# First norm's roots on every partition, from dense sums, in a two-layer decoder trunk

## The chip, the cores and the metric

The kernel runs on one core of a Trainium2 chip. The metric is the device time of one execution in microseconds (us); the span of a profile is the time between its first and last instruction, and the execution's own time is a little longer than the span. Engines are named as in the profile: PE (TensorE, with PEld for its weight loads), ACT (ScalarE), DVE (VectorE), POOL (GpSimd) and SP (SyncE, which here issues the DMAs).

## The reference

Two pre-norm residual layers over 256 tokens of width 1024. Layer 0 mixes tokens with forgetting attention, layer 1 with block-sparse attention; each is followed by a SwiGLU FFN and a gated embedding, and a last norm ends it. What matters here is the norm and its first use:

```python
def _rmsnorm(x, g):
    x32 = x.astype(jnp.float32)
    y = x32 * lax.rsqrt(jnp.mean(x32 * x32, axis=-1, keepdims=True) + RMS_EPS)
    return (y * g.astype(jnp.float32)).astype(x.dtype)
...
u = _rmsnorm(h, attn_norm_g[i])
...
proj = u @ fox_w_in[j]
q, k, v = _heads(proj[..., :D]), _heads(proj[..., D:2 * D]), _heads(proj[..., 2 * D:3 * D])
f_logit = proj[..., 3 * D:].astype(jnp.float32) + fox_b_f[j].astype(jnp.float32)
log_f = jax.nn.log_sigmoid(f_logit).transpose(0, 2, 1)
```

There are seven norms: three in each layer (before the mixer, the FFN and the embedding's gate) and the last one. The kernel numbers them 0 to 6.

## The kernel before, in words

The hidden state is held transposed in `hx`: 128 partitions by 8 blocks of features by 256 tokens. So a token's sum of squares runs over partitions, and a root per token is wanted in two shapes: as a row (the same 256 numbers on every partition, `row`) for results that have tokens along the free axis, and as a column (`col`, 128 tokens on the partitions, two columns) for results that have tokens on partitions. The norm's gain is put onto the input before the products, the root onto their results: products of queries, keys, values and gates start before the root is known.

Products are made in a three-fold split: each float32 operand is a high part (`whi`, made by ACT, line 186 or 162) and a low part (`wlo`, made by DVE, line 187 or 167), and `mm3` (lines 96 to 100) adds three products. Weights stream in as 216 blocks of 128 x 1024 (`half`, lines 142 to 188). SP issues their DMAs into six buffers `raw`, ACT and DVE split them into six pairs `whi` and `wlo`, and PE uses them in the order of the text. The tile framework puts each engine's instructions into an order by a planner of its own, by readiness and priority; so an instruction can stand elsewhere on ACT, DVE or SP than the text has it. Waits are semaphores, and each engine takes its instructions in the planned order.

Layer 0's attention (`attention`, lines 437 to 585) begins with the values: 8 feature blocks k, each 12 products into four PSUM banks (`v`, in four units of a token half and a column half). In between come:

- after k = 3, `nm.square(0)` and `nm.square(1)` (lines 222 to 237): ACT squares `hx`, DVE adds up to `ss`, 128 x 256, one partial sum per partition and token;
- at k = 5, first unit: `fox_bias` (line 359) makes the forget gates' products (`pf`), with exact float32 operands, and `nm.root()`;
- at k = 6, third unit: `nm.spread(-0.125)`, and `rest()` (line 375), which multiplies the gates by the root's row, makes their logarithms, runs them along the tokens, writes them to DRAM (`cd`) and reads them back onto all partitions (`bias`); POOL adds the mask there;
- after k = 7, the values are taken out of PSUM with `col` (lines 479 to 485), and the query and key blocks (`project`, line 493) follow, whose results are multiplied by `rows()`.

A norm's root is made in two ways. Norms 1 to 4 (`ROWS`, line 38) use `by_rows` (lines 260 to 281): `ss` is split into `sh`, two products with a matrix of ones (`every`) put the whole sum onto all partitions, ACT makes the root there, and ACT and DVE make one correcting step. Norm 3, the one ahead of layer 1's attention, also has the row times -0.125, and gets `col` by multiplying the row with the unit matrix and adding up (line 280). Norm 0 uses the text of `root` (lines 246 to 258): tiny products of `ss` with one column of ones give the sums with tokens on partitions, DVE scales them, POOL raises them to the power -1/2 (`col`), ACT and DVE make two split diagonal matrices of it (`dg`), and `spread` (lines 286 to 296) multiplies `every` with these, so that the root's row stands on all partitions, and copies it out twice.

`table(func, after)` (line 108) runs a one-element activation so that ACT loads the table of a function ahead of its first use; `after` makes it wait for a value.

Of the kernel before, what the change touches and what calls it, by code (L numbers as in the profile page):

```python
# [13 lines left out]
ALU = mybir.AluOpType  # L14
# [20 lines left out]
GN = 64  # L35
CST = 528
EARLY = 4
ROWS = (1, 2, 3, 4)
VISITS = (((), (), ()), ((), (0, 1, 2), ()), ((0, 1, 2), (3, 4), (0, 1, 2)), ((3, 4), (5, 6, 7), (3, 4)))
XK = ((0, 1, 0), (1, 2, 2), (2, 3, 3), (3, 4, 4), (4, 8, 4))  # L40

# [38 lines left out]
def trunk(ctx: ExitStack, tc: tile.TileContext, pt, w, cst, gf, out):  # L80
# [7 lines left out]
    def bank(name):  # L88
        return ps.tile([P, 512], F32, tag="bank", name=name)
# [18 lines left out]
    def table(func, after=None):  # L108

        nc.scalar.activation(warm, ones if after is None else after, func)  # L110
# [10 lines left out]
        nc.sync.dma_start(gx[:, GN + k0 * S:GN + k1 * S], packed(w, x_at(c), (k1 - k0) * S))  # L121

    nc.scalar.dma_start(gx[:, 0:GN + S], packed(w, 0, GN + S))
    table(AF.Square)

    eps = first_line[:, 24:25]
    nc.gpsimd.memset(eps, EPS)
# [71 lines left out]
    class Norm:  # L199
# [22 lines left out]
        def square(self, hf):  # L222

            for m in (4 * hf, 4 * hf + 2):
                src = hx[:, m:m + 2].rearrange("p m s -> p (m s)")
                if m == 0:
                    self.ss = work.tile([P, HC], F32, tag="ss", bufs=1, name=f"ss{self.n}")
                    nc.scalar.activation(self.ss, src, AF.Square)
                    continue
                sq = work.tile([P, HC], F32, tag="t2k", bufs=3, name=f"sq{self.n}_{m}")  # L230
                nc.scalar.activation(sq, src, AF.Square)
                nc.vector.tensor_tensor(self.ss, self.ss, sq, op=ALU.add)
            if hf:
                nc.vector.tensor_tensor(self.ss[:, 0:S], self.ss[:, 0:S], self.ss[:, S:2 * S], op=ALU.add)
                if self.n in ROWS:
                    self.sh = work.tile([P, 2, S], F32R, tag="t2k", bufs=3, name=f"sh{self.n}")
                    split(self.sh[:, 0], self.sh[:, 1], self.ss[:, 0:S])

        def root(self):

            n = self.n
            pr = self.pr = bank(f"pr{n}")
            if n in ROWS:
                self.by_rows(pr)
                return
            ms = tiny.tile([P, 2], F32, tag="ms", name=f"ms{n}")
            for t in range(2):
                mm(pr[:, S + t:S + t + 1], self.ss[:, t * P:(t + 1) * P], ones, start=True, stop=True)
            nc.vector.tensor_scalar(ms, pr[:, S:S + 2], 1.0 / D, EPS, op0=ALU.mult, op1=ALU.add)
            self.col = tiny.tile([P, 2], F32, tag="col", name=f"col{n}")  # L250
            nc.gpsimd.tensor_tensor(self.col, ms, nhalf, op=ALU.pow)
            self.dg = work.tile([P, 2, S], F32R, tag="t2k", bufs=3, name=f"dg{n}")
            at = [slice(t * P, (t + 1) * P) for t in range(2)]
            for t in range(2):
                nc.scalar.activation(self.dg[:, 0, at[t]], ident, AF.Copy, scale=self.col[:, t:t + 1])
            for t in range(2):
                nc.vector.scalar_tensor_tensor(self.dg[:, 1, at[t]], ident, self.col[:, t:t + 1], f32(self.dg[:, 0, at[t]]),
                                               op0=ALU.mult, op1=ALU.subtract)

        def by_rows(self, pr):  # L260

# [20 lines left out]

        def rows(self):
            return self.row if self.n % 3 == 0 else self.row[:, 1:2].to_broadcast([P, 2, S])

        def spread(self, scale=1.0):

            n = self.n
            if n in ROWS:
                return  # L290
            pr = self.pr
            for i in range(2):
                mm(pr[:, 0:S], every, self.dg[:, i], start=i == 0, stop=i == 1, skip_group_check=True)
            self.row = work.tile([P, 2, S], F32, tag="row", name=f"row{n}")
            nc.scalar.activation(self.row[:, 0], pr[:, 0:S], AF.Copy, scale=scale)
            nc.vector.tensor_copy(self.row[:, 1], pr[:, 0:S])

        def k(self, m):
            return self.hi[:, m], self.lo[:, m]
# [57 lines left out]


    def fox_bias(nm):
        table(AF.Exp)  # L360
        nc.vector.tensor_tensor(fg[:, :, 0:H], wf32, gn[:, 0].unsqueeze(2).to_broadcast([P, KT, H]), op=ALU.mult)
        pf = bank("pf")
        groups = P // GC
        for k in range(KT - groups, -1, -groups):
            for g in range(groups):
                mm(pf[GC * g:GC * g + GC, :S], fg[:, k + g], hx[:, k + g], start=(k == KT - groups), stop=(k == 0),
                   skip_group_check=True)

        parts = [work.tile([H, S], F32, tag="pt", bufs=6, name=f"fparts{g}") for g in range(1, groups)]
        for g in range(1, groups):  # L370
            nc.scalar.activation(parts[g - 1], pf[GC * g:GC * g + H, :S], AF.Copy)
        for g, q in enumerate(parts):
            nc.vector.tensor_tensor(parts[0], pf[:H, :S] if g == 0 else parts[0], q, op=ALU.add)

        def rest():
            with tc.high_priority():
                f = work.tile([H, S], F32, tag="pt", bufs=6, name="f")
                nc.vector.tensor_tensor(f, parts[0], nm.row[:H, 1], op=ALU.mult)
                nc.vector.tensor_scalar(f, f, bfs, None, op0=ALU.add)
                a = work.tile([H, S], F32, tag="pt", bufs=6, name="fabs")  # L380
                nc.scalar.activation(a, f, AF.Abs)
                nc.scalar.activation(a, a, AF.Exp, scale=-1.0)
                nc.scalar.activation(a, a, AF.Ln, bias=1.0)
                nc.vector.scalar_tensor_tensor(f, f, 0.0, a, op0=ALU.min, op1=ALU.subtract)
                cum = work.tile([H, S], F32, tag="pt", bufs=6, name="cum")
                nc.vector.tensor_tensor_scan(cum, f, zero, 0.0, ALU.add, ALU.add)
                cd = dram.tile([H, S], F32, name="cd")
                nc.scalar.dma_start(cd, cum)
            both = work.tile([P, H * 3 * P], F32, tag="bias", bufs=1, name="bias0")
            c, first = both[:, 0:H * S].rearrange("p (h s) -> p h s", s=S), both[:, H * S:].rearrange("p (h s) -> p h s", s=P)  # L390
            for h0, h1 in ((0, 4), (4, 10), (10, 16)):
                nc.sync.dma_start(both[:, h0 * S:h1 * S],
                                  bass.AP(tensor=cd.tensor, offset=cd.offset + h0 * S, ap=[[0, P], [1, (h1 - h0) * S]]))
            for i in range(H):
                nc.gpsimd.tensor_tensor(first[:, i], c[:, i, 0:P], mask, op=ALU.add)
                nc.gpsimd.tensor_tensor(c[:, i, P:S], c[:, i, P:S], mask, op=ALU.add)
            return lambda i: (first[:, i], c[:, i])

        return rest
# [37 lines left out]
    def attention(layer, nm, mid, early, nf):  # L437
        vb = [bank(f"v{layer}_{b}") for b in range(4)]
        for c in range(4):
            wt = [early.pop(0) if early else half() for _ in range(2)]  # L440
            for kk in range(2):
                hi, lo = wt[kk]
                k = 2 * c + kk
                if layer == 1 and k == 3:
                    nm.turn(1)
                    nm.square(1)
                units = [(t, hf) for hf in range(2) for t in range(2)]
                if layer == 0 and k < 3:
                    for part, n in ((part, n) for part in (units[0:2], units[2:4]) for n in range(3)):
                        x, wt_ = ((nm.hi, hi), (nm.lo, hi), (nm.hi, lo))[n]  # L450
                        for t, hf in part:
                            mm(vb[2 * t + hf], x[:, k, t * P:(t + 1) * P], wt_[:, hf * HC:(hf + 1) * HC],
                               start=(k == 0 and n == 0), stop=False, skip_group_check=True)
                else:
                    for t, hf in units:
                        if layer == 0 and k == 5 and (t, hf) == units[0]:
                            rest = mid(nm)
                            nm.root()
                        if layer == 0 and k == 6 and (t, hf) == units[2]:
                            nm.spread(-0.125)  # L460
                            bias = rest()
                        cols = slice(hf * HC, (hf + 1) * HC)
                        tokens(vb[2 * t + hf], nm.k(k), t, (hi[:, cols], lo[:, cols]), k == 0, k == KT - 1)
                if layer == 0 and k == 3:
                    nm.square(0)
                    nm.square(1)
                if layer == 0 and k == 5:
                    distances()
# [5 lines left out]
                nm.root()  # L474
                table(AF.Exp, nm.y)
        if layer == 1:
            nm.spread(-0.125)
            bias = mid(nm)()
        for hf in range(2):
            for t in range(2):  # L480
# [485 lines left out]
```

## Time and profile before

| What | us |
|---|---|
| median of 3 runs (643.43 to 643.61) | 643.6 |
| the profiled execution | 643.48 |
| its span | 641.7 |
| PE busy in the span | 633.4 |
| PEld busy | 612.2 |
| DVE busy | 453.2 |
| ACT busy | 375.8 |
| POOL busy | 31.6 |

In the rows of a timeline the columns are start, length, engine, line, operation, tiles (out<-in), shapes and count, with the idle time before and what ended it in brackets. Lengths of products overlap, as the next begins before the last has left the array. Rows of groups end in busy time, mean length of one in ns, and idle time before them. Rows of the chain of waits are start, length and what stood on the chain.

### The profile page before, as it was taken

What the parts mean: (1) busy time and instruction counts of PE and PEld (TensorE: products, weight loads), DVE (VectorE), ACT (ScalarE), POOL (GpSimd) and SP (SyncE); (2) the same over time, 40 slices, a digit from 0 to 9 for tenths busy, and PEclk for the clock granted to TensorE, in tenths of its full rate; (3) what the DMA queues carried; (4) which work ended last, traced back from release to release, by engine and by line L of the source; (5) the groups of instructions that cost most, each with busy time, mean ns of one, the idle gap of its engine ahead of it and who ended that gap; (6) DMA issues with size and microseconds to landing.
All of it is one profiled execution on the core that took longest, in us unless ns stands there. A gap on an engine that the chain in (4) does not pass through costs nothing.

```text
span 641.7 us, 13157 instructions
## 1 busy us (share of the span) xinstructions
PE 633.4 (99%) x5303; PEld 612.2 (95%) x5303; DVE 453.2 (71%) x782; ACT 375.8 (59%) x659; POOL 31.6 (5%) x66
## 2 busy tenths in 40 slices
PE   9999999999999999999999999999999999999995
PEld 7899999999999999999989999999999999999985
DVE  6877975786666666658896687678766666666665
ACT  8746775764444445448876486568444444454772
POOL 2337000000000000000000000000000000000002
PEclk9999999999999999999999999999999999999999
DMA  9889834376566566565687544435765566666501
GB/s 325 305 272 339 266 130 158 106 254 206 194 195 198 195 191 207 191 192 172 208 276 257 178 154 132 132 102 176 252 198 194 198 197 197 195 207 192 180 1 66
DMA packets 36941, 124.93 MB, mean 195 GB/s; under 512 B 3952, under 2 KB 6800, under 8 KB 36880
## 3 DMA queue, kind: packets, MB, share of 16 engines
q1 hardware_dynamic: 36560, 123.65, 58.4%
q8 instruction: 41, 0.67, 0.4%
q10 hardware_dynamic: 320, 0.44, 0.2%
q14 instruction: 20, 0.16, 0.1%
HBM read 122.99 MB, written 4.24 MB: 198 GB/s over the span
## 4 chain that ended last, share of the span: by engine, by line
PE 97%; DMA 1%; POOL 0%; issue 0%; ACT 0%; DVE 0%; POOLq 0%; DVEq 0%
PE gu L99 12%; PE gu L100 12%; PE gu L98 12%; PE fo L99 6%; PE fo L100 6%; PE fo L98 6%; PE pq L98 5%; PE pq L100 5%; PE pq L99 5%; PE wo L98 2%; PE wo L100 2%; PE wo L99 2%; PE pg L99 2%; PE pg L100 2%; PE pg L98 2%; PE v L98 2%
## 5 line engine op out<-in xcount | busy, mean ns | idle before, releaser
L187 DVE TENSOR_TENSOR wlo<-raw,whi 128x1024 fp32r<-128x1024 f32 (+1 forms) x198 | 237.5, 1204 | 109.9 <-ACT whi L186 104.4
L186 ACT ACTIVATE whi<-raw 128x1024 fp32r<-128x1024 f32 (+1 forms) x198 | 205.4, 1041 | 151.7 <-issue 57.2
L99 PE MATMUL gu<-g,whi 128*128 128x256 f32 x702 | 193.8, 276 | 0.0
L98 PE MATMUL gu<-g,whi 128*128 128x256 f32 x702 | 193.8, 276 | 0.0
L100 PE MATMUL gu<-g,wlo 128*128 128x256 f32 x702 | 193.8, 276 | 0.0
L98 PEld LDWEIGHTS gu<-g,whi 128*128 128x128 f32 x702 | 131.8, 188 | 0.0
L100 PEld LDWEIGHTS gu<-g,wlo 128*128 128x128 f32 x702 | 131.8, 188 | 0.0
L99 PEld LDWEIGHTS gu<-g,whi 128*128 128x128 f32 x702 | 131.8, 188 | 0.0
L98 PE MATMUL fo<-fh,whi 128*128 128x256 f32 x352 | 97.3, 276 | 0.0
L100 PE MATMUL fo<-fh,wlo 128*128 128x256 f32 x352 | 97.2, 276 | 0.0
L99 PE MATMUL fo<-fl,whi 128*128 128x256 f32 x352 | 97.2, 276 | 0.0
L98 PE MATMUL pq<-g,whi 128*128 128x256 f32 x256 | 71.3, 278 | 0.0
L100 PE MATMUL pq<-g,wlo 128*128 128x256 f32 x256 | 70.9, 277 | 0.0
L99 PE MATMUL pq<-g,whi 128*128 128x256 f32 x256 | 70.9, 277 | 0.0
L98 PEld LDWEIGHTS fo<-fh,whi 128*128 128x128 f32 x352 | 66.1, 188 | 0.0
L99 PEld LDWEIGHTS fo<-fl,whi 128*128 128x128 f32 x352 | 66.1, 188 | 0.0
L100 PEld LDWEIGHTS fo<-fh,wlo 128*128 128x128 f32 x352 | 66.1, 188 | 0.0
L98 PEld LDWEIGHTS pq<-g,whi 128*128 128x128 f32 x256 | 48.1, 188 | 1.1 <-issue 0.3
L100 PEld LDWEIGHTS pq<-g,wlo 128*128 128x128 f32 x256 | 48.2, 188 | 0.0
L99 PEld LDWEIGHTS pq<-g,whi 128*128 128x128 f32 x256 | 48.1, 188 | 0.1
L327 ACT ACTIVATE fh<-sg 128x256 fp32r<-128x256 f32 x44 | 18.1, 415 | 49.5 <-DVE sg L631 49.5
L167 DVE TENSOR_TENSOR wlo<-raw,whi 128x256 fp32r<-128x256 f32 (+3 forms) x44 | 29.9, 689 | 13.9 <-ACT whi L162 13.9
(178 smaller groups left out, 982.5 us busy)
## 6 DMA issues: line engine op xcount, KB each, us to landing
raw<-w SPq DMA_DIRECT2D x212, 512.0 KB, 4.2
d<-d SPq DMA_DIRECT2D x4, 768.0 KB, 10.3
raw<-w SPq DMA_DIRECT2D x8, 256.0 KB, 4.6
bias<-d SPq DMA_DIRECT2D x4, 512.0 KB, 7.3
bias<-cd SPq DMA_DIRECT2D x2, 768.0 KB, 7.9
gx<-w SPq DMA_DIRECT2D x1, 512.0 KB, 5.5
bias<-cd SPq DMA_DIRECT2D x1, 512.0 KB, 3.9
p<-pt SPq DMA_DIRECT2D x2, 256.0 KB, 4.2
```

The costliest lines, as they stand in the source:

```text
L98: mm(o, ah, bh, start=start, stop=False, skip_group_check=True)
L99: mm(o, ah, bl, start=False, stop=False, skip_group_check=True)
L100: mm(o, al, bh, start=False, stop=stop, skip_group_check=True)
L167: nc.vector.tensor_tensor(t[:, a + b0 * P:a + b1 * P], raw[:, b0 * P:b1 * P], f32(ht[:, a0:a0 + (b1 - b0) * P]), op=ALU.subtract)
L186: nc.scalar.activation(hi[:, c], raw[:, c], AF.Copy)
L187: nc.vector.tensor_tensor(lo[:, c], raw[:, c], f32(hi[:, c]), op=ALU.subtract)
L327: nc.scalar.activation(hi, src, AF.Copy)
```

## The change

All norms that use `root` now use `by_rows`. The list `ROWS` goes, and with it the tiny products, the power on POOL, the diagonals and `spread`. Norm 0's sums are split into `sh` like those of norms 1 to 4, and since 0 is divisible by 3 it gets the row times -0.125 and the columns like norm 3. In layer 0 the root moves from the first to the third unit of k = 5; what `spread` did at k = 6 falls away, `rest()` stays there. The first table that ACT loads is that of the reciprocal root in place of Square's, and Exp's is asked for behind the root, on the value `nm.y`, in place of inside `fox_bias`.

```diff
-ROWS = (1, 2, 3, 4)
...
-    table(AF.Square)
+    table(AF.Abs_reciprocal_sqrt)
...
-                if self.n in ROWS:
+                if self.n < 5:
                     self.sh = work.tile([P, 2, S], F32R, tag="t2k", bufs=3, name=f"sh{self.n}")
                     split(self.sh[:, 0], self.sh[:, 1], self.ss[:, 0:S])
...
         def root(self):
 
-            n = self.n
-            pr = self.pr = bank(f"pr{n}")
-            if n in ROWS:
-                self.by_rows(pr)
-                return
-            ms = tiny.tile([P, 2], F32, tag="ms", name=f"ms{n}")
-            for t in range(2):
-                mm(pr[:, S + t:S + t + 1], self.ss[:, t * P:(t + 1) * P], ones, start=True, stop=True)
-            nc.vector.tensor_scalar(ms, pr[:, S:S + 2], 1.0 / D, EPS, op0=ALU.mult, op1=ALU.add)
-            self.col = tiny.tile([P, 2], F32, tag="col", name=f"col{n}")
-            nc.gpsimd.tensor_tensor(self.col, ms, nhalf, op=ALU.pow)
...
-                nc.scalar.activation(self.dg[:, 0, at[t]], ident, AF.Copy, scale=self.col[:, t:t + 1])
...
+            self.by_rows(bank(f"pr{self.n}"))
...
-        def spread(self, scale=1.0):
...
-                mm(pr[:, 0:S], every, self.dg[:, i], start=i == 0, stop=i == 1, skip_group_check=True)
...
     def fox_bias(nm):
-        table(AF.Exp)
...
                         if layer == 0 and k == 5 and (t, hf) == units[0]:
                             rest = mid(nm)
+                        if layer == 0 and k == 5 and (t, hf) == units[2]:
                             nm.root()
+                            table(AF.Exp, nm.y)
                         if layer == 0 and k == 6 and (t, hf) == units[2]:
-                            nm.spread(-0.125)
                             bias = rest()
...
         if layer == 1:
-            nm.spread(-0.125)
             bias = mid(nm)()
```

More of the change, by code (lines that the diff above doesn't have):

```diff
@@ L239, in root @@
         def root(self):
-            n = self.n
-            pr = self.pr = bank(f"pr{n}")
-            if n in ROWS:
-                self.by_rows(pr)
-                return
-            ms = tiny.tile([P, 2], F32, tag="ms", name=f"ms{n}")
-            for t in range(2):
-                mm(pr[:, S + t:S + t + 1], self.ss[:, t * P:(t + 1) * P], ones, start=True, stop=True)
-            nc.vector.tensor_scalar(ms, pr[:, S:S + 2], 1.0 / D, EPS, op0=ALU.mult, op1=ALU.add)
-            self.col = tiny.tile([P, 2], F32, tag="col", name=f"col{n}")
[L251 to L258, printed above, removed]
+            self.by_rows(bank(f"pr{self.n}"))
         def by_rows(self, pr):
@@ L284, in rows @@
             return self.row if self.n % 3 == 0 else self.row[:, 1:2].to_broadcast([P, 2, S])
-        def spread(self, scale=1.0):
[L288 to L296, printed above, removed]
         def k(self, m):
```

## The prediction

> **What bounds the kernel now.** I read the page first (busy shares and the chain that ended last), then TensorE's own waits, and then the instructions of the 15 us in which the first norm's root is made, one engine at a time. The page's rows:
>
> ```profile
> span 641.7 us, 13157 instructions
> PE 633.4 (99%) x5303; PEld 612.2 (95%) x5303; DVE 453.2 (71%) x782; ACT 375.8 (59%) x659; POOL 31.6 (5%) x66
> ...
> PE 97%; DMA 1%; POOL 0%; issue 0%; ACT 0%; DVE 0%; POOLq 0%; DVEq 0%
> ```
>
> The table of who waited for whom, of TensorE alone over the whole span, has one entry once weights flow (the other is 0.8 us of warming up):
>
> ```profile
> PE v L452 <- ACT whi L186: 0.5, 1, 0.5
> ```
>
> The reader is to see that TensorE waits for nobody after the first 5 us. So the only thing this change can save is TensorE time itself, and the only thing it can lose is a wait that TensorE doesn't have today. In the timeline of TensorE (start, length, line, tiles) the old root stands in two places, and the form that replaces it already stands at the FFN's norm:
>
> ```profile
> 19.87 0.61 PE L248 MATMUL pr<-first_line,ss 128*128 128x1 f32 x4
> 20.34 0.48 PE L98 MATMUL v<-whi,g 128*128 128x512 f32 x1
> ...
> 21.82 0.39 PE L98 MATMUL v<-whi,g 128*128 128x512 f32 x1
> ...
> 24.55 0.51 PE L293 MATMUL pr<-dg,every 128*128 128x256 f32 x2
> 24.89 0.40 PE L98 MATMUL v<-whi,g 128*128 128x512 f32 x1
> ...
> 26.49 0.39 PE L99 MATMUL v<-wlo,g 128*128 128x512 f32 x1
> ...
> 28.98 0.28 PE L98 MATMUL pq<-g,whi 128*128 128x256 f32 x1
> ...
> 123.59 0.39 PE L264 MATMUL pr<-sh,every 128*128 128x256 f32 x2
> 123.81 0.28 PE L98 MATMUL gu<-g,whi 128*128 128x256 f32 x1
> ```
>
> Lengths overlap in the pipeline, so I count from start to start: what a group takes is the next start minus its own. The chain of waits gives a second reckoning of the same groups:
>
> ```profile
> 19.94 0.54 PE pr L248 x4
> ...
> 24.71 0.34 PE pr L293 x2
> ...
> 336.52 0.24 PE pr L264 x2
> ```
>
> **TensorE, removed and added.** The tiny products (L248, two in the code, four in the trace) go: 20.34 - 19.87 = 0.47. The spread over the diagonals (L293) goes: 24.89 - 24.55 = 0.34. The two dense products with `every` (L264) come, at k = 5's third unit: 123.81 - 123.59 = 0.22. The sum is 0.47 + 0.34 - 0.22 = 0.59 us less. By the chain it is 0.54 + 0.34 - 0.24 = 0.64. A lower end comes from the weight loads:
>
> ```profile
> L248 PEld LDWEIGHTS pr<-first_line,ss 128*128 128x128 f32 x4 | 0.5, 190 | 0.4 <-DVE wlo L187 0.4
> ```
>
> The weight loader stood 0.4 us before L248 and the chain has TensorE on the gates' product until 19.94; if the next value product can't start before that either, L248's place is worth 20.34 - 19.94 = 0.40 and the sum is 0.40 + 0.34 - 0.24 = 0.50. I take 0.6, where the two full reckonings meet, with 0.50 and 0.64 as ends; even with the new products at nothing it would be 0.54 + 0.34 = 0.88.
>
> A rule of the Trainium skill speaks against most of this: the page "TensorE: Matmul & The Clock Gate", section "Back-to-back issue gap", has products of 1 to 64 columns leave about 25 ns apart, so four tiny ones would be worth an estimated 0.10, and the sum by that rule would be 0.10 + 0.34 - 0.22 = 0.22 (643.3 in place of 642.9). The row decides otherwise: the four take 0.47, 0.12 each. The same page, section "LDWEIGHTS (loading the stationary operand)", explains it, as it has a weight load cost its columns over 1.2 per ns, 107 ns for 128, and these products load 128 columns each.
>
> **ScalarE and VectorE: what the new form needs, and when.** ScalarE's rows in the stretch, then VectorE's:
>
> ```profile
> 2.46 0.44 ACT L110 ACTIVATE first_line<-first_line 128x1 f32<-128x1 f32 x2
> ...
> 20.06 1.16 ACT L371 ACTIVATE fparts<-pf 16x256 f32<-16x256 f32 x3 [2.52 <-PE pf L366]
> 21.12 1.04 ACT L186 ACTIVATE whi<-raw 128x1024 fp32r<-128x1024 f32 x1
> 22.42 0.70 ACT L255 ACTIVATE dg<-cs,col 128x128 fp32r<-128x128 f32 x2 [0.26 <-POOL col L251]
> 23.02 1.14 ACT L162 ACTIVATE whi<-raw 128x256 fp32r<-128x256 f32 x2
> ...
> 125.88 0.40 ACT L270 ACTIVATE ry<-ry 128x256 f32<-128x256 f32 x1
> 126.29 1.28 ACT L110 ACT_TABLE_LOAD   x1
> 127.59 0.20 ACT L110 ACTIVATE first_line<-ry 128x1 f32<-128x1 f32 x1
> ```
>
> ```profile
> 18.26 0.41 DVE L234 TENSOR_TENSOR ss<-ss 128x256 f32<-128x256 f32 x1
> 18.60 1.21 DVE L187 TENSOR_TENSOR wlo<-raw,whi 128x1024 fp32r<-128x1024 f32 x1
> ...
> 21.70 0.88 DVE L373 TENSOR_TENSOR fparts<-fparts,fparts 16x256 f32<-16x256 f32 x2
> 22.86 0.35 DVE L257 SCALAR_TENSOR_TENSOR dg<-cs,col,dg 128x128 fp32r<-128x128 f32 x1 [0.28 <-ACT dg L255]
> 23.13 1.22 DVE L187 TENSOR_TENSOR wlo<-raw,whi 128x1024 fp32r<-128x1024 f32 x1
> ...
> 24.52 1.29 DVE L167 TENSOR_TENSOR wlo<-raw,whi 128x256 fp32r<-128x256 f32 x2
> 25.73 0.42 DVE L296 COPY row<-pr 128x256 f32<-128x256 f32 x1
> ```
>
> The prices of the added steps stand at the other norms, by tile (min/median/max in ns):
>
> ```profile
> L269 ACT ACTIVATE ry<-pr,first_line x4: 452/455/457, 124.6 to 437.3; 128x256 f32<-128x256 f32 x4
> ...
> L271 DVE SCALAR_TENSOR_TENSOR ry<-pr,ry x4: 418/418/420, 127.2 to 439.9; 128x256 f32<-128x256 f32 x4
> ...
> L272 DVE TENSOR_SCALAR ry<-ry x4: 293/294/295, 127.6 to 440.3; 128x256 f32<-128x256 f32 x4
> L273 DVE TENSOR_TENSOR row<-ry x4: 425/426/426, 127.9 to 440.6; 128x256 f32<-128x256 f32 x4
> L280 DVE CUSTOM_DVE_ANT_0 ry<-row,cs x2: 288/292/296, 340.7 to 341.0; 128x128 f32<-128x128 f32 x2
> ```
>
> ```profile
> L327 ACT ACTIVATE sh<-ss x4: 395/418/419, 120.2 to 432.9; 128x256 fp32r<-128x256 f32 x4
> ```
>
> The low half takes 0.41 (L328, quoted with the rivals).
>
> *The split of the sums.* They are whole at 18.26 + 0.41 = 18.67. ScalarE is idle from 17.54 to 20.06 (the 2.52), so the high half costs nothing there (0.42, done at about 19.1). VectorE is on a weight block until 19.81; the low half would then be done at 19.81 + 0.41 = 20.22. TensorE comes to the new products at the seventh value product of k = 5, 21.82 - 0.47 = 21.35: 1.1 us of cover. If that is used up, TensorE itself stands, one for one.
>
> *The root chain.* The sum is out by 21.35 + 0.39 = 21.74; ScalarE ends its weight block at 22.16, makes the root (0.46) and its square (0.40) by 23.0; VectorE, free at 22.58, can do the next weight block (1.22) and then 0.42 + 0.29 + 0.43 = 1.14, so the row stands at about 24.9 and the columns (two of 0.29) at 25.5. Today the row stands at 25.73 + 0.42 = 26.15. So the gates, their trip through memory and the bias, which hang on the row, come no later, and no DMA is added or passed. VectorE gains 0.41 + 1.14 + 0.58 = 2.13 and loses 0.70 (two L257) and 0.42, some 1.0 more; ScalarE gains 0.46 + 0.40 + 1.28 + 0.20 and loses 0.70, 1.64 more (the copy to `row` stays), the Exp load being new there: today Square and Exp are both warmed at 2.46, one right behind the other.
>
> *What hides it.* What waits behind these queues is the split of the weights. The block of k = 7 has its low part at 23.13 + 1.22 = 24.35 and TensorE reads it at 26.49, which becomes 25.90: today's cover of 2.1 is 1.5 after the shift, less VectorE work put in front of it. The first query block (L162, L167) has its low part at 25.81; later by ScalarE's 1.64 it is 27.45, against TensorE at 28.98 - 0.59 = 28.39: 0.9 left. Both hold, so I cost these edits at nothing; bounds are 0 and the full loss of cover, which the rivals price. That a block can come out earlier gives TensorE nothing.
>
> The Trainium skill would cut the second cover: "ScalarE: Activation LUTs", section "What ACT_TABLE_LOAD costs", adds a drain of about 1.38 us to a load of 1.28, which by my estimate would put that low part at 28.8, past 28.39. Here the trace disagrees: the load starts 0.01 us after the square's end and the next activation 0.02 us after the load's, so no drain shows, and the rival that it would feed gets no more than its chance below.
>
> *The rest at nothing.* The first table load serves another function in the same place, before any data; one of the two warming activations at 2.46 goes; GpSimd loses its tiny power; the bank is held from 21.35 instead of from 19.87.
>
> **The sum.** 643.48 for the profiled execution (span 641.7, 1.8 around it) less 0.6 is 642.9. The median of the runs is 643.6, 0.12 above that execution, so I say 643.0.
>
> **Rivals.** *The gain is waited away.* Issue order is not text order. In layer 1 the same split came late on VectorE, behind three weight pieces:
>
> ```profile
> 331.49 0.41 DVE L234 TENSOR_TENSOR ss<-ss 128x256 f32<-128x256 f32 x1
> ...
> 334.17 0.41 DVE L328 TENSOR_TENSOR sh<-ss,sh 128x256 fp32r<-128x256 f32 x1
> ```
>
> That is 2.68 from start to start; here it would end the split at 18.26 + 2.68 + 0.41 = 21.35, just as TensorE arrives. Behind the gates' additions (21.70 + 0.88 = 22.58) it would end at 23.0, a wait of 1.65 and 643.0 + 1.65 = 644.6; with half of that, 643.8. For it: that row. Against it: VectorE is idle from 19.81 in this stretch, with no weight block to put in front until 23.13.
>
> *The new chain stalls the k = 7 block: slower.* VectorE serves in order. If the root's first VectorE step is issued ahead of that block's low part and ScalarE makes the root only after two more weight blocks (22.16 + 1.14 + 1.04 = 24.34, plus 0.46 + 0.40), the step starts at 25.2, the chain with the columns ends at 25.2 + 1.14 + 0.58 = 26.9, and the block at 28.1; TensorE, there at 25.90, stands 2.2: 645.2. It decides from 25.90 on, and is slower than before from 26.5. Against it: the block's high part is ready at 22.16, before the root can be, so it should come first.
>
> *The tiny products were not on the path.* If TensorE's place at 19.87 is set by something else, only 0.34 - 0.24 = 0.10 is left: 643.5.
>
> **How the numbers follow.** About 0.2%, 1.3 us, is what a measurement here can tell from no change: below 642.3 or above 644.9. Forecast 0.66; gain waited away 0.13; not on the path 0.05; the stalled block 0.11. Faster by over 0.2% would need more than the 0.88 that is there to remove, so only an unseen reordering gives it: 0.05. That is 0.84 for the same. The range, 642.5 to 644.2, leaves out the stalled block, the 0.05 and the worst of the waiting.
>
> **What would show it.** Right: TensorE's waits still have only the first entries; L248 and L293 are gone, L264 has ten products; L264 to the next start is 0.22 to 0.24 near 21.3; the query blocks begin near 28.4. Wrong: a wait of `pr` on `sh` (first rival) or of `v` L99 on `wlo` (second), a gap before the first value product after the gates' product (third), or a changed order of blocks later on.

## The result and the profile after

The changed kernel takes 650.2 us (median of 22 runs, 643.45 to 652.1) against 643.5 us for the kernel before (22 runs on the same chip): a ratio of 1.007, 95% interval 1.0051 to 1.0089. The forecast of 643.0, with a range of 642.5 to 644.2, was wrong. The 22 times fall into two groups, 9 from 643.45 to 644.82 and 13 from 649.67 to 652.1, so the median is that of the larger group and no single amount. The profiled execution, of 652.1 us, is of the upper group. Rows of its page:

```profile
span 650.3 us, 13154 instructions
PE 636.7 (98%) x5299; PEld 614.8 (95%) x5299; DVE 458.8 (71%) x786; ACT 378.0 (58%) x661; POOL 26.7 (4%) x65
...
PEclk9997999999999999999999999999999999999999
```

TensorE's own waits, which had nothing over 0.8 us before:

```profile
PE sp L479 <- DVE qkt L469: 5.9, 1, 5.9
PE cold L130 <- PEq L927: 0.8, 1, 0.8
```

There is one new wait, of 5.9 us, at the scores of a pair of heads, 29 us behind the changed products. First the changed part. The timeline of TensorE of before, two rows that the prediction did not need, and then of after:

```profile
18.87 1.07 PE L366 MATMUL pf<-gx,fg 128*32 128x256 f32 x16
...
50.87 2.24 PE L510 MATMUL sp<-qkt 64*128 64x128 f32 x24
```

```profile
19.44 1.07 PE L335 MATMUL pf<-gx,fg 128*32 128x256 f32 x16
20.44 0.50 PE L97 MATMUL v<-whi,g 128*128 128x512 f32 x1
...
21.96 0.39 PE L246 MATMUL pr<-sh,every 128*128 128x256 f32 x2
22.18 0.40 PE L97 MATMUL v<-whi,g 128*128 128x512 f32 x1
...
29.01 0.28 PE L97 MATMUL pq<-g,whi 128*128 128x256 f32 x1
29.13 0.28 PE L98 MATMUL pq<-g,whi 128*128 128x256 f32 x1
...
50.90 1.58 PE L479 MATMUL sp<-qkt 64*128 64x128 f32 x16
58.34 1.65 PE L479 MATMUL sp<-qkt 64*128 64x128 f32 x8 [5.86 <-DVE qkt L469]
60.30 0.42 PE L98 MATMUL pq<-g,whi 128*128 128x256 f32 x1
60.51 0.41 PE L99 MATMUL pq<-g,wlo 128*128 128x256 f32 x1
```

From the gates' product to the first query product it was 28.98 - 18.87 = 10.11 and is 29.01 - 19.44 = 9.57: 0.54 less, as the prediction's term had it. (The gates' product itself starts 0.57 later here than in the profile before; the same program has it at 18.68 in the profile of its second run, `after_again` below, so that is not the change.) The loss comes between 50.90 and 58.34, and TensorE isn't up to speed after it. The windows of that stretch (columns: window, its length, busy time of PE, PEld, DVE, ACT and POOL with their counts, granted clock, DMA share, GB/s):

```profile
52.00:56.00 4.00, 0.48 (x6) 0.07 (x2) 4.00 (x1) 2.52 (x3) 4.00 (x11) 1.00 0.27 108
56.00:60.00 4.00, 1.67 (x9) 1.01 (x9) 4.00 (x5) 0.00 (x0) 0.60 (x2) 0.71 0.26 85
60.00:62.00 2.00, 2.00 (x9) 2.00 (x10) 2.00 (x9) 0.54 (x3) 0.00 (x0) 0.50 0.83 244
62.00:64.00 2.00, 2.00 (x11) 2.00 (x11) 2.00 (x8) 1.51 (x7) 0.00 (x0) 0.50 0.88 330
64.00:66.00 2.00, 2.00 (x17) 2.00 (x17) 2.00 (x12) 1.23 (x7) 0.00 (x0) 0.87 0.86 248
66.00:70.00 4.00, 4.00 (x37) 4.00 (x37) 3.43 (x17) 4.00 (x13) 0.00 (x0) 1.00 0.88 312
```

The granted clock falls to 0.50 late in TensorE's stop and stays there until about 64.5: query products leave 60.51 - 60.30 = 0.21 apart instead of 29.13 - 29.01 = 0.12. From 60 to 66 there are 9 + 11 + 17 = 37 products, as many as in the four microseconds after: 2 us lost beside the wait. From the first scores to the end of the span it is 650.3 - 50.90 = 599.4 here and was 641.7 - 50.87 = 590.8 before: 8.6, of which 5.9 are the wait and 2 or more the slow clock. (The Trainium skill, "TensorE: Matmul & The Clock Gate", part 1 on the clock gate, has half clock after an idle window of about 3.4 us; the trace agrees with it: 5.9 us idle, granted 0.50.) So long a stop isn't needed for it, though: in the run `after_qkt` below the clock was granted at 0.53 from 72 to 74 us, and no stop ahead of that was longer than 1.63 us.

Why is `qkt`, the queries and keys of that pair times the root's row, late? VectorE, then GpSimd (two of 32 mask additions that run one behind the other without a gap, the first and the last), then ScalarE:

```profile
41.39 1.20 DVE L186 TENSOR_TENSOR wlo<-raw,whi 128x1024 fp32r<-128x1024 f32 x1
49.57 8.11 DVE L186 TENSOR_TENSOR wlo<-raw,whi 128x1024 fp32r<-128x1024 f32 x1 [6.98 <-ACT whi L185]
57.60 0.68 DVE L469 TENSOR_TENSOR qkt<-pq,row 128x512 f32<-128x512 f32 x1
```

```profile
43.29 0.46 POOL L364 TENSOR_TENSOR bias<-bias,cs 128x128 f32<-128x128 f32 x1 [21.60 <-DMA bias<-cd]
...
56.14 0.46 POOL L365 TENSOR_TENSOR bias<-bias,cs 128x128 f32<-128x128 f32 x1
```

```profile
48.47 1.07 ACT L185 ACTIVATE whi<-raw 128x1024 fp32r<-128x1024 f32 x1 [7.40 <-DMA raw<-w]
```

The low part of one weight block, 1.20 us elsewhere, takes 8.11: it starts at 49.57, amid the additions, and ends at 57.68, 1.08 after the last of them (56.14 + 0.46 = 56.60). It stands ahead of `qkt`, and the scores wait for `qkt`. And it is late to begin with (before, the same low part started at 43.80 and took 1.22), since ScalarE had waited 7.40 us for the block's DMA. SP's queue says why; before, then after:

```profile
35.23 0.33 SPq L183 DMA_DIRECT2D raw<-w  x1
39.01 2.20 SPq L392 DMA_DIRECT2D bias<-cd  x3
```

```profile
34.54 0.33 SPq L182 DMA_DIRECT2D raw<-w  x1
36.49 1.28 SPq L361 DMA_DIRECT2D bias<-cd  x3
37.87 1.00 SPq L182 DMA_DIRECT2D raw<-w  x2
```

The three transfers that bring the gates' bias back from memory (16 heads by 256 tokens of float32 on 128 partitions, 2 MB) now stand ahead of two weight blocks, numbers 18 and 19 (the queries and keys of pair 5), behind which they stood before. Nothing else on SP has moved, and TensorE's order is the same but for the changed products. What the bias hangs on is ready earlier: the write of `cd` is issued at 33.43 and was at 35.80. That the planner of the tile framework, which orders by readiness, let the transfers go first for this reason is a reading; no run tests why it moved them.

```profile
35.80 0.33 ACTq L388 DMA_DIRECT2D cd<-cum  x1
```

```profile
33.43 0.33 ACTq L357 DMA_DIRECT2D cd<-cum  x1
```

The kernel before has the same meeting of VectorE and GpSimd, without harm: VectorE is let in between two additions, and it is an addition that waits.

```profile
46.57 1.54 DVE L187 TENSOR_TENSOR wlo<-raw,whi 128x1024 fp32r<-128x1024 f32 x1 [0.34 <-ACT whi L186]
```

```profile
46.97 1.45 POOL L396 TENSOR_TENSOR bias<-bias,cs 128x128 f32<-128x128 f32 x1
```

The Trainium skill, "SBUF — State Buffer", section "Who interferes with whom", has a VectorE instruction with two inputs in SBUF share a port with a GpSimd instruction that reads SBUF, and the later one wait until the other has finished. That is the 1.45 above, and it would cost VectorE at most one addition of 0.46; a wait over the 16 additions that follow is not in that rule.

So the theory is a chain: an earlier row, bias transfers ahead of two weight blocks, a low part that asks amid GpSimd's additions and is at times held to the last of them, a late `qkt`, a stop and a slow clock. Its rivals were B, that the new root costs something by itself; and C, that the late blocks cost it and GpSimd has no part.

### The profile page after: what moved, and what is told of

It reads as the page before. It is cut to its first block, busy times and chain, and to the rows that moved or that the text cites. A ratio compares the mean times of both kernels' runs of the same rounds, so it can differ in the third digit from the quotient of the medians.

```text
span 650.3 us, 13154 instructions
## 1 busy us (share of the span) xinstructions
PE 636.7 (98%) x5299; PEld 614.8 (95%) x5299; DVE 458.8 (71%) x786; ACT 378.0 (58%) x661; POOL 26.7 (4%) x65
## 4 chain that ended last, share of the span: by engine, by line
PE 97%; issue 1%; POOL 0%; DVE 0%; ACT 0%; POOLq 0%; DVEq 0%
PE gu L97 12%; PE gu L98 12%; PE gu L99 12%; PE fo L98 6%; PE fo L99 6%; PE fo L97 6%; PE pq L97 5%; PE pq L98 5%; PE pq L99 5%; PE wo L97 2%; PE wo L98 2%; PE wo L99 2%; PE pg L99 2%; PE pg L98 2%; PE pg L97 2%; PE v L97 2%
## 5 line engine op out<-in xcount | busy, mean ns | idle before, releaser
L186 DVE TENSOR_TENSOR wlo<-raw,whi 128x1024 fp32r<-128x1024 f32 (+1 forms) x198 | 243.8, 1236 | 114.8 <-ACT whi L185 109.2
L97 PE MATMUL pq<-g,whi 128*128 128x256 f32 x256 | 72.3, 282 | 0.0
L98 PE MATMUL pq<-g,whi 128*128 128x256 f32 x256 | 71.8, 280 | 0.0
L97 PEld LDWEIGHTS pq<-g,whi 128*128 128x128 f32 x256 | 49.1, 192 | 1.4 <-issue 1.0
L98 PEld LDWEIGHTS pq<-g,whi 128*128 128x128 f32 x256 | 49.1, 192 | 0.1
L597 DVE TENSOR_TENSOR gut<-gu,row 128x512 f32<-128x512 f32 x44 | 30.2, 691 | 11.9 <-PE gu L99 11.8
```

Of the source, the lines that this page charges most:

```text
L97: mm(o, ah, bh, start=start, stop=False, skip_group_check=True)
L98: mm(o, ah, bl, start=False, stop=False, skip_group_check=True)
L186: nc.vector.tensor_tensor(lo[:, c], raw[:, c], f32(hi[:, c]), op=ALU.subtract)
L597: nc.vector.tensor_tensor(t, bks[f].rearrange("p (a s) -> p a s", s=S), nm.rows(), op=ALU.mult)
```

## The experiments

### The changed kernel once more

No edit.

> The changed kernel once more, unaltered, to see how its times spread beside the three others on the same chip. Theory A (SyncE issues the three gate-bias transfers ahead of two weight blocks; the low part of the first of these then starts late, inside GpSimd's 32 mask additions, and VectorE is held until GpSimd is done; the scores' input stands behind it on VectorE): two groups of times, about 644 and 650.5, by whether VectorE is let in between two additions. Theory B (the new root's own steps on ScalarE and VectorE are late): one group near 650. Theory C (the two weight blocks land late, GpSimd plays no part): one group near 650, or times in between by the landing.

Measured: median 650.99 (643.05, and five from 650.91 to 651.96), ratio to before 1.01, 1.0064 to 1.0136. The profiled execution happens to be the one of 643.05 us, span 641.3. The same program, the same order, and TensorE has no wait but the 0.8 of warming up; the first rows are VectorE's, the last GpSimd's:

```profile
48.42 1.60 DVE L186 TENSOR_TENSOR wlo<-raw,whi 128x1024 fp32r<-128x1024 f32 x1 [6.59 <-ACT whi L185]
49.95 0.68 DVE L469 TENSOR_TENSOR qkt<-pq,row 128x512 f32<-128x512 f32 x1
```

```profile
48.90 1.44 POOL L364 TENSOR_TENSOR bias<-bias,cs 128x128 f32<-128x128 f32 x1
```

The block is as late as in the other profile (6.59 idle against 6.98), but the low part is let in at the second boundary, and takes 1.60. That is what sets these two profiles, one of each group, apart: spans of 650.3 and 641.3.

### Only SP's order put back

The changed kernel, with the three bias transfers issued behind block 19 as before; no other instruction moves.

```diff
...
+            if i == BEHIND:
+                for ins in state["bias"]:
+                    tc.add_manual_dep(ins, weights.ins.name, ...)
...
```

> The changed kernel with one thing put back: SyncE issues the three gate-bias transfers behind the same two weight blocks as in the kernel before; no other instruction changes its place on any engine. Theory A: the wait of 5.9 us on the scores is gone in all runs, and what is left is the shorter TensorE work, 642.6 to 643.2 against 643.5 before. Theory B: the wait stays, 650. Theory C: as theory A, the two are not told apart here.

Measured: 642.71 (642.2 to 643.52, 11 runs) against 643.59 for before; ratio 0.999, 0.9981 to 0.9999. Block 18 is there in time:

```profile
43.88 1.23 DVE L191 TENSOR_TENSOR wlo<-raw,whi 128x1024 fp32r<-128x1024 f32 x1 [1.23 <-ACT whi L190]
```

TensorE has no wait but the 0.8 of warming up. B falls: the whole new root is in this kernel, and it is no slower than before, if anything 0.9 faster, where 0.5 to 0.6 were expected of the products. This is the fastest version among these runs that leaves nothing out. The lower group of the changed kernel doesn't reach it: the median of its nine times is 644.2, against 642.7 here. So the order seems to cost something in the lower group too; no profile of the changed kernel at such a time was kept, and where it goes is not shown.

### Only SP's order changed, in the kernel before

The old root, with the order of the changed kernel on SP around the bias. Two further pins, not shown, keep `qkt` of pair 2 (pairs count from 0) on VectorE and a later transfer on SP in their places; in the trace nothing but the bias and the two blocks has moved.

```diff
...
+                with tc.issue_after(state["bias"].ins) if layer == 0 and j == 5 else nullcontext():
+                    hi, lo = blocks(form=FORMS.get((layer, a, j)))
...
```

> The kernel before, its old root untouched, with SyncE's order of the changed kernel: the three gate-bias transfers ahead of the same two weight blocks; all else keeps its place. Theory A (the order on SyncE makes the low part late, GpSimd holds VectorE): slower though no root is changed; the bias leaves at about 39, later than in the changed kernel, so the first block lands near 50 and its low part is ready at 51.5 at best, the scores' input at 52.2: 644 to 645 where VectorE is let in, 649 to 654 where it is held. Theory B (the new root's steps): 643.5, nothing changes.

Measured: 647.24 (8 runs: four of 643.04 to 644.91, four of 649.57 to 651.35), ratio 1.006, 1.0024 to 1.0097. The profiled execution:

```profile
PE sp L515 <- DVE qkt L505: 4.8, 1, 4.8
```

```profile
49.35 7.54 DVE L187 TENSOR_TENSOR wlo<-raw,whi 128x1024 fp32r<-128x1024 f32 x1 [6.74 <-ACT whi L186]
```

The order alone, with no product changed, makes the same held low part, the same wait, and both groups of times. So the loss goes with the order from both sides: with the old order the changed kernel doesn't have it, with the new one the old kernel does.

### GpSimd's additions left out

The changed kernel without the mask additions, so the causal mask is missing from layer 0's attention; the bias is used as it comes.

```diff
-            for i in range(H):
-                nc.gpsimd.tensor_tensor(first[:, i], c[:, i, 0:P], mask, op=ALU.add)
-                nc.gpsimd.tensor_tensor(c[:, i, P:S], c[:, i, P:S], mask, op=ALU.add)
-            return lambda i: (first[:, i], c[:, i])
+            return lambda i: (c[:, i, 0:P], c[:, i])
```

> The changed kernel without GpSimd's 32 additions of the causal mask to the gate bias: this leaves the causal mask out of layer 0's attention; the scores read the transferred bias directly. Order on the other engines is unaltered. Theory A: nothing holds VectorE, the low part takes 1.2 us from its landing at about 49.6, the scores' input is ready near 51.5, TensorE waits 0.3 to 1.0 in place of 5.9: one group, 643.2 to 644.2. Theory B and C: the wait stays as it is, 650.

Measured: 642.58 (642.38 to 643.35, 11 runs), ratio 0.9987, 0.9978 to 0.9995; TensorE has no wait but the 0.8 of warming up.

```profile
48.98 1.23 DVE L186 TENSOR_TENSOR wlo<-raw,whi 128x1024 fp32r<-128x1024 f32 x1 [7.21 <-ACT whi L185]
```

The block is just as late (7.21 idle) and it costs nothing, less than the 0.3 to 1.0 that I expected. C falls: late blocks have their cover, and it takes GpSimd's additions to make a stop of it.

### `qkt` of pair 2 taken out from behind the held block

The changed kernel, SP's order as changed, with pair 5's low parts behind `qkt` of pair 2 on VectorE.

```diff
+                with tc.issue_after(state["qkt0_2"].ins) if (layer, a, j) == (0, 0, 5) else nullcontext():
+                    hi, lo = blocks(form=FORMS.get((layer, a, j)))
```

> The changed kernel with one place altered on VectorE: the third pair's scaled queries and keys are made ahead of the low part of the weight block that is late, not behind it. SyncE's order stays as changed. Theory A: the low part is still held by GpSimd in some runs, until about 57, but TensorE needs it only at about 57 to 58, so all runs lie at 642.7 to 644.0. Theory B: 650, since the root's steps are untouched. Theory C: as theory A within 0.5.

Measured: 649.13 (648.28 to 650.39, 4 runs), ratio 1.0089, 1.0076 to 1.0102. A miss: 642.7 to 644.0 was expected. VectorE, and the two longest of TensorE's waits (with two shorter ones they sum to 3.2):

```profile
44.62 0.69 DVE L470 TENSOR_TENSOR qkt<-pq,row 128x512 f32<-128x512 f32 x1 [2.97 <-PE pq L99]
49.31 8.23 DVE L186 TENSOR_TENSOR wlo<-raw,whi 128x1024 fp32r<-128x1024 f32 x2 [4.00 <-ACT whi L185]
58.67 0.68 DVE L470 TENSOR_TENSOR qkt<-pq,row 128x512 f32<-128x512 f32 x1
```

```profile
PE pq L97 <- DVE qkt L470: 1.6, 1, 1.6
PE sp L480 <- ACT pt L508: 0.9, 1, 0.9
```

Pair 2's `qkt` does go ahead, amid the additions, at its usual 0.69; it has one input in PSUM, and it wasn't held. But the two blocks are held as before, and now `qkt` of pair 3 and the softmax stand behind them. To the waits comes a slow clock, 0.53 from 72 to 74 us. The wait goes to the next in the queue: it is the hold that must go, not one of its victims.

### A one-element fill behind each addition

The changed kernel; GpSimd writes one unused element after each mask addition.

```diff
+                    with tc.issue_after(add.ins):
+                        done = nc.gpsimd.memset(first_line[:, 16:17], 0.0)
```

> The changed kernel with a one-element fill behind each of GpSimd's 32 mask additions, which writes and reads nothing; order elsewhere unaltered. Theory A1 (VectorE is held because the additions follow each other without a break in their reads): VectorE is let in at the first such break, all runs 642.4 to 643.5. Theory A2 (GpSimd keeps VectorE out as long as its queue is not empty): still two groups, or all near 651 since the run of additions is 3 us longer.

Measured: 643.58 (642.74 to 644.68, 11 runs), ratio 1.0002, 0.9993 to 1.0011: one group. The low part takes 1.37 at 48.42. In the profile the fill that follows, at 48.56, is where VectorE seems to come in: the next addition is stretched to 1.49.

### A one-element addition in place of the fill

```diff
-                        done = nc.gpsimd.memset(first_line[:, 16:17], 0.0)
+                        done = nc.gpsimd.tensor_tensor(first_line[:, 16:17], mask[:, 0:1], mask[:, 0:1], op=ALU.add)
```

> The same with a one-element addition, which reads, in place of the fill. Theory A1: two groups as in the changed kernel, 643 and 651, since the reads still follow each other. Theory A2: two groups or all near 651. If any extra boundary is a chance to get in: all runs near 643 here and with the fills.

Measured: 645.13 (12 runs, 644.13 to 649.06; all but three between 644.1 and 645.6), ratio 1.0032, 1.0018 to 1.0047. If only an instruction that doesn't read let VectorE in, this would have had the changed kernel's two groups. It hasn't: a short instruction that reads helps nearly as often, though the median is 1.5 us above that with fills. So it isn't settled what the fill does.

### Fills ahead of the asking, and behind it

Two kernels tell where a fill has to stand: behind the first ten additions alone, or behind the last twelve alone.

```diff
-                if n < 10:
+                if n >= 20:
                     with tc.issue_after(done.ins):
                         done = nc.gpsimd.memset(first_line[:, 16:17], 0.0)
```

> The changed kernel with a one-element fill on GpSimd behind each of the first ten of its 32 mask additions and none behind the other 22. So every boundary of the other kind has passed before block 18's low part asks at about 49.5 us, some five additions later. Theory E1 (what counts is a boundary of the other kind after VectorE has asked): nothing changes, two groups of times as in the changed kernel (642.7 to 645 and 649.5 to 652), and a profiled execution of the second group has a low part of 7 to 8 us. Theory E2 (what counts is how many additions have run without a break before VectorE asks; the kernel before asks after two and is always let in): one group, 642.7 to 644.8, and the low part at most 1.7 us. At least 4 of 11 executions in the upper group speak for E1, none for E2.

> The same with the fills behind the last twelve additions alone, from the 21st on, which ends at about 51.9 us; VectorE asks at about 49.5, in the middle of 21 additions without a break. Theory E1 (a boundary of the other kind lets VectorE in whenever it comes): where it is held it comes in at the first fill, so that the low part takes about 2.4 + 1.2 = 3.6 us and ends near 53.2; TensorE then waits about 5.9 - (57.7 - 53.2) = 1.4 us, so the upper group stands at about 644 to 646 in place of 649.5 to 652. Theory E2 (once held, held to the last addition): two groups as in the changed kernel, and a low part of 8 us in a profiled execution of the upper one.

Measured, fills ahead: 650.54 (10 runs: three of 643.36 to 644.02, seven of 650.47 to 651.43), ratio 1.0082, 1.0051 to 1.0114. Two groups, as without fills; the low part of the profiled execution is held for 7.77. VectorE asked there after some six additions without a break, and it was held about as often as after 15 (13 of 22). In the kernel before, a shorter low part asks in the seventh in a row, at 51.11, and is let in. So it isn't the number of additions without a break that decides (E2 falls). Fills behind: 645.83 (12 runs), ratio 1.0049, 1.002 to 1.0078; eight from 643.48 to 645.99, most of them where E1 had them, and four from 650.67 to 652.67, where E1 had none. One of the four was profiled:

```profile
49.04 8.28 DVE L186 TENSOR_TENSOR wlo<-raw,whi 128x1024 fp32r<-128x1024 f32 x1 [7.02 <-ACT whi L185]
```

The fills begin at 51.23 in it and VectorE comes in at none of them. So E1 in its strict form falls too. That a fill behind the asking helps in some executions is likely but not shown: three times of 645.81 to 645.99 lie where the changed kernel has none, and no profile of them was kept; 4 of 12 in the upper group against 13 of 22 are too few to tell apart. What decides in one execution whether VectorE is let in or held to the end stays open: the moment within the running addition is no rule, since in the profiles it was held when it asked 0.02 us (`after_behind18`) and 0.28 us (`after_qkt`) behind the start of one and let in at 0.02 (`before`) and 0.36 (`after_again`).

### Only one of the two blocks put back

`BEHIND` = 18: block 18 ahead of the bias transfers, block 19 still behind them.

> The changed kernel with one of the two weight blocks put back ahead of the gate-bias transfers on SyncE, the other left behind them. Theory A: the first block's low part is made in time and the scores' third input with it; the second's is held by GpSimd in some runs, and the fourth pair's input and the softmax of the first heads stand behind it on VectorE: two groups, 642.7 and 648 to 650. Theory D (only the first late block matters): one group, 642.7.

Measured: 642.82 (11 of 12 from 642.12 to 644.3, one of 650.03), ratio 0.9991, 0.9983 to 1.0. The one of 650.03 is the profiled one: there it is block 19 that is held.

```profile
50.76 7.76 DVE L191 TENSOR_TENSOR wlo<-raw,whi 128x1024 fp32r<-128x1024 f32 x1 [5.08 <-ACT whi L190]
```

So D, that only the first late block matters, falls by one execution: either low part can be held. Why it was held in only one of 12 here, and in 13 of 22 of the changed kernel, is open.

## Why the prediction was wrong

*TensorE's term was right.* 0.59 less was forecast, within 0.50 to 0.64, and 0.54 was found (9.57 against 10.11). The two dense products take 22.18 - 21.96 = 0.22, as taken from the FFN's norm. L248's place went whole: from the gates' product to the next value product it was 20.34 - 18.87 = 1.47 and is 20.44 - 19.44 = 1.00. The weight loader's lower reckoning (0.40) was not needed, and the rival that the tiny products were not on the path is out.

*The split of the sums and the root chain went as forecast.* TensorE waits neither for `sh` nor for `wlo` in this stretch, so the first rival and that of the block of k = 7 did not come. VectorE's and ScalarE's rows:

```profile
19.80 0.41 DVE L298 TENSOR_TENSOR sh<-ss,sh 128x256 fp32r<-128x256 f32 x1
...
25.22 0.43 DVE L255 TENSOR_TENSOR row<-ry 128x256 f32<-128x256 f32 x1
25.68 0.41 DVE L347 TENSOR_TENSOR f<-fparts,row 16x256 f32<-16x256 f32 x1
```

```profile
23.86 1.28 ACT L109 ACT_TABLE_LOAD   x1
25.16 0.20 ACT L109 ACTIVATE first_line<-ry 128x1 f32<-128x1 f32 x1
```

The low half is done at 20.21 (forecast 20.22), the row at 25.65 (forecast 24.9, and the gates' product, ahead of it all, starts 0.57 later in this profile), and Exp's table load has nothing behind it that would be a drain: 23.86 + 1.28 = 25.14, then 25.16.

*The step that failed* is the one sentence "So the gates, their trip through memory and the bias, which hang on the row, come no later, and no DMA is added or passed", and with it the edits costed at nothing. The first half holds: they come earlier, the write of `cd` by 2.4 us. From that the second half doesn't follow, and it is false: the three bias transfers passed two weight blocks on SP. What the runs showed in place of nothing is some 6 to 9 us in 13 of 22 executions: a wait of 5.9 us of the scores and 2 or more of slow clock, which go when the order alone is put back (642.71) and come when the order alone is changed in the old kernel (647.24, four of 8 from 649.57). I looked for what could come late and asked of nothing what it does when it comes early; the sentence "That a block can come out earlier gives TensorE nothing" has the same gap. The prediction names "a changed order of blocks later on" among the signs of an error, but gives it no price, and none of the rivals has GpSimd in it: the 0.11 for slower was another mechanism.

*The price* could not have been read from the trace of before: there the low parts of 128 x 1024 that meet the additions take 1.54 at most, and the additions stretch to 1.48. That a meeting can cost 8 us is in no row of it. But that a mask addition and a low part can stretch each other stood there, and a sum over the moved transfers would have found two late blocks with only their cover to protect them. That cover held where the additions were left out, so it takes the hold, which no row of before shows, to make the loss.

## What to carry to other kernels

When a change makes a value come earlier, list the transfers that hang on it, and look at what stands behind each in its queue under a planner that orders by readiness; pin that order if the value isn't urgent. Keep VectorE's instructions with two inputs in SBUF out of a long run of GpSimd additions, or break up the run, if something on the path stands behind them. Where the times of one program fall into two groups, compare two of its own profiles before any other.

## What the runs showed of the hardware

A VectorE subtraction with both inputs in SBUF that asked amid GpSimd's additions of 0.46 us was let in within two of them (1.22 to 1.60 us in all) or held until the last, 7.54 to 8.28 us against 1.2; one and the same program had 1.60 in one execution and 8.11 in another. A VectorE product with one input in PSUM took its usual 0.69 amid them. With one element written on GpSimd behind each addition none of 11 executions was in the upper group; with fills behind the first ten alone it was 7 of 10, with fills behind the last twelve alone 4 of 12. And a stop of 5.9 us cost TensorE some 2 us more, as its clock was granted at 0.50 until about 64.5 us, 6 us after it had begun again; after waits of 1.6, 0.5, 0.2 and 0.9 us within some 12 us the clock was at 0.53 as well (`after_qkt`).
